# Queries, keys and u of an encoder layer: tokens stationary, 512 weight columns moving, then a turn on TensorE

## The chip, the cores and the metric

The kernel runs on one core of a Trainium2 chip. The metric is the device time of one execution in microseconds, the median of several runs. A core has five engines that are used here: TensorE (PE; its weight loads are listed apart as PEld), VectorE (DVE), ScalarE (ACT), GpSimd (POOL) and SyncE (SP), which issues the transfers from HBM. Each engine works through its own instructions in a fixed order and waits on semaphores for the others. TensorE writes to PSUM, which has eight banks of 128 partitions by 512 float32 here; four of them form two accumulators of 1024 columns, four are single banks.

## What is computed

One layer of an encoder on 256 tokens of width 2048, in float32. Cut to what matters here:

```python
h = rmsnorm(x, norm1_g)
z = h @ w_in                      # (256, 2048) @ (2048, 9216)
u_a, v_a, q, k, v_b, gate_logits = jnp.split(z, splits, axis=-1)   # u, v, q, k, v_b: 1024 columns each
a = spatial_gating(u_a, v_a, ...)                 # u = gelu(u); v = layernorm(gelu(v)); u * (W_s v + b_s)
o = diff_attention(q, k, v_b, lam, slopes)        # 8 heads, two score maps each, softmax(p0) - lam * softmax(p1)
gates = sigmoid(gate_logits + b_gate)
x = x + (gates[0] * (a @ w_proj_a) + gates[1] * (rmsnorm(o) @ w_proj_b)) @ w_out
x = x + hier_moe(rmsnorm(x), ...)                 # 16 experts, top 2 of the best group; final norm
```

## The kernel before

All weights are streamed from HBM once, in blocks of 128 x 2048 float32 (1 MB), in the order of use, into 27 "slots" of that size in SBUF, which activations share. A slot is given back when its content has been used, and the stream takes the slot that has been idle longest; a transfer waits until the last reader of its slot is done. SP issues all transfers in one order.

Products are made from two levels: every weight block is split by ScalarE and VectorE into a high part (`L85`, a cast) and a low part (`L86`, what is left), into a ring of three buffers, half a block at a time. The normalized tokens are kept in the same way (`hh`, `hl`). A product is then three matmuls: high by high, and each high by the other's low.

`z = h @ w_in` is made in groups of 512 columns. A group reads four blocks, 16 steps of 128 rows of the weights (k-steps). There are two forms:

- `cols_group` (lines 255 to 269, for queries, keys and u): 128 weight columns are stationary and the 256 tokens move (`L264`). A step is 12 matmuls of 256 columns, a group 192. The result has columns of z on the partitions and tokens along the free axis, as attention and the gating want it. VectorE multiplies it by the norm's factor `rb` (one per token, copied to all partitions): `L316`, `L325`, `L401`.
- `toks_block` (lines 271 to 281, for v_b, v, the gates, and later projections): 128 tokens are stationary and 512 weight columns move (`L280`). A step is 6 matmuls of 512 columns, a group 96. The result has tokens on the partitions; the norm's factor is a scalar per partition (`rcol`, made from `rb` by two tiny matmuls `L251`).

The groups come in the order q0, k0, v_b0, q1, k1, v_b1, v0, v1, u0, u1, then eight groups of gates. Queries and keys are written in two levels (`q2`, `k2`, `kl`; `L319`, `L320`, `L328` to `L330`). Between the groups the code starts the eight attention heads (`head`, lines 342 to 377): eight score matmuls (`L349`, `L350`), a softmax on VectorE and ScalarE in two buffers s0 and s1, four transposes (`L368`, wT), a split into wh and wl, six matmuls (`L375`, oT). s0, s1, wh, wl and other temporaries come from the pool `wk`, which has two buffers and hands them out in the order of the code. The spatial gating follows (`L420`, "mixed"), on u.

A scheduler orders each engine's instructions when the program is built: the code's order sets which buffers follow which, and an instruction comes up as soon as the scheduler thinks its inputs ready. After head 7 the slots of queries and keys are given back; the gates' biases (`L518`, bias_rows, four transfers to one of these slots) and the sixth and following blocks of the gates' weights go there.

Of the kernel before, what the change touches and what calls it, by code (L numbers as in the profile page):

```python
# [9 lines left out]
F32 = mybir.dt.float32  # L10
# [3 lines left out]
AF = mybir.ActivationFunctionType  # L14
OP = mybir.AluOpType
# [3 lines left out]
S = 256  # L19
NK = D // 128  # L20
# [76 lines left out]
def encoder(ctx, tc, A, out, stop=None):  # L97
    nc = tc.nc
    V, SC, PE, GP = nc.vector, nc.scalar, nc.tensor, nc.gpsimd
# [62 lines left out]
    stream = Stream(nc, slots, blocks)  # L162
# [40 lines left out]
    ident = consts.tile([128, 128], F32, name="ident")  # L203
# [15 lines left out]
    hh = [t[0].rearrange("p (k t) -> p k t", k=8) for t in hTh]  # L219
    hl = [t[0].rearrange("p (k t) -> p k t", k=8) for t in hTl]  # L220
    rb = dead_tile((S,))
    rcol = consts.tile([128, 2], F32, name="rcol")

    def x_in(c):

        half = xT[c // 4][0][:, c % 4 * 512:c % 4 * 512 + 512]
        nc.sync.dma_start(half, A["xT"].rearrange("p k t -> p (k t)")[:, c * 512:(c + 1) * 512])
        for k in range(2 * c, 2 * c + 2):
            i, kk = divmod(k, 8)
            SC.activation(hh[i][:, kk], xv[i][:, kk], AF.Copy, scale=g1[:, k:k + 1])  # L230
            V.scalar_tensor_tensor(hl[i][:, kk], xv[i][:, kk], g1[:, k:k + 1], hh[i][:, kk].bitcast(F32),
                                   op0=OP.mult, op1=OP.subtract)
# [19 lines left out]
                      skip_group_check=True)  # L252
        V.tensor_copy(rcol, rp[:, :2])

    def cols_group(xh, xl, nk, n_blocks, first_of_all=False):

        ps = acc()
        for b in range(n_blocks):
            for k, wh, wl in stream.parts((lambda k: x_in(2 * b + k // 2)) if first_of_all else None, first_of_all and b == 0):
                kk = b * 4 + k  # L260
                a, al = xh[kk // 8][:, kk % 8], xl[kk // 8][:, kk % 8]
                for w, v, first in ((wh, a, True), (wh, al, False), (wl, a, False)):
                    for j in range(4):
                        PE.matmul(ps[:, j * S:(j + 1) * S], w[:, j * 128:(j + 1) * 128], v,  # L264
                                  start=kk == 0 and first and j % 2 == 0,
                                  stop=kk == nk - 1 and w is wl and j % 2 == 1, skip_group_check=True)
        if first_of_all:
            x_norm()
        return ps.rearrange("p (j t) -> p j t", j=4)

    def toks_block(ps, xh, xl, b, nb):

        for k, wh, wl in stream.parts():
            kk = b * 4 + k
            a, al = xh[kk // 8][:, kk % 8], xl[kk // 8][:, kk % 8]
            steps = [(v, w, t) for v, w in ((a, wh), (a, wl), (al, wh)) for t in range(2)]
            if kk == nb * 4 - 1:
                steps.sort(key=lambda s: s[2])
            for v, w, t in steps:
                PE.matmul(ps[:, t * 512:(t + 1) * 512], v[:, t * 128:(t + 1) * 128], w,  # L280
                          start=kk == 0 and v is a and w is wh, stop=kk == nb * 4 - 1 and v is al)

    rb4 = rb[:, None, :].to_broadcast([128, 4, S])

    def z_cols(first_of_all=False):
        return cols_group(hh, hl, NK, 4, first_of_all)

    def toks_group(xh, xl, nb):

        ps = acc()  # L290
        for b in range(nb):
            toks_block(ps, xh, xl, b, nb)
        return ps.rearrange("p (t n) -> p t n", t=2)

    def z_toks():
        return toks_group(hh, hl, 4)

    view = lambda s, k: s[0].rearrange("p (k n) -> p k n", k=k)

# [3 lines left out]
    half = slice(0, 64), slice(64, 128)  # L303
    heads = slots.take()
    oT = view(heads, 8)
# [5 lines left out]
    vh, vl = view(vhs, 2), view(vls, 2)  # L311

    def evac_q(i):
        c = slice(4 * i, 4 * i + 4)
        q = oT[:, c]
        V.tensor_tensor(q, z_cols(i == 0), rb4, op=OP.mult)  # L316
        for m in range(2):
            a, b = half[m], half[1 - m]
            SC.copy(q2[m][a, c], q[a])  # L319
            V.tensor_tensor(q2[m][b, c], q[a], q2[m][a, c].bitcast(F32), op=OP.subtract)  # L320

    def evac_k(i):
        c = slice(4 * i, 4 * i + 4)
        k = oT[:, c]
        V.tensor_tensor(k, z_cols(), rb4, op=OP.mult)  # L325
        for m in range(2):
            a, b = half[m], half[1 - m]
            SC.copy(k2[m][a, c], k[a])  # L328
            SC.copy(k2[m][b, c], k[a])
            V.tensor_tensor(kl[m][a, c], k[a], k2[m][a, c].bitcast(F32), op=OP.subtract)  # L330

    def evac_vb(i):
        ps = z_toks()
# [627 lines left out]
```

## Time and profile before

| | |
|---|---|
| median of 3 runs | 1084.84 us (1083.54 to 1085.14) |
| the profiled execution | 1083.54 us |
| its span, first to last instruction | 1081.6 us |
| TensorE with work | 1048.3 us, 97% |
| weight loads | 700.1 us, 65% |
| VectorE, ScalarE | 510.0 us (47%), 395.9 us (37%) |
| read from HBM | 320.25 MB, 298 GB/s over the span |
| first half (norm, z, attention, gating, projections) | to about 622 us |
| experts | from about 630 us |

The rows that are shown below name an instruction by its line, engine, operation and operands (out<-in), with a count (x) and times in microseconds, or nanoseconds where it says so. "Busy" of TensorE counts a matmul to a modelled end, and matmuls overlap; how fast they follow each other is read from their starts. In square brackets stands how long the engine was idle before, and whom it waited for.

### The profile page before, as it was taken

Reading aid. Unit: us, or ns where it says so; the run is one execution under the profiler, and the core shown is the slowest. Engines: PE = TensorE matmul, PEld = TensorE weight load, DVE = VectorE, ACT = ScalarE, POOL = GpSimd, SP = SyncE. Lnnn points to the kernel's source line nnn. Section 1 sums busy time; section 2 is a strip of 40 time slices with the busy share of each in tenths; the row PEclk is TensorE's granted clock in tenths of the full one; section 3 lists DMA queues with packets and bytes.
Section 4 is the critical chain, followed back from the end, with each engine's and each line's share of the span. In section 5 each row is a group of like instructions: output and inputs, shape, how many; then the busy total and the mean of one; then the engine's idle time right before and its main releaser. Section 6 shows DMA issues by size and latency. Waiting matters only on the chain. (4 is left out here: it accounts for less than half of the span.)

```text
span 1081.6 us, 13529 instructions
## 1 busy us (share of the span) xinstructions
PE 1048.3 (97%) x5436; PEld 700.1 (65%) x5436; DVE 510.0 (47%) x745; ACT 395.9 (37%) x554; POOL 9.1 (1%) x16
## 2 busy tenths in 40 slices
PE   7999999999999999999999999999999998999995
PEld 7989988998788888888887743444434432333331
DVE  8775676866778655566655541312313111122121
ACT  7564555555566444444443320211211101111112
POOL 1000000000000000000000000000000000000000
PEclk9999999999999999999999999999999999999997
DMA  9914455455875656556964769999999999999994
GB/s 338 420 61 171 156 197 190 158 209 181 272 265 191 228 192 231 191 203 248 364 254 160 299 269 422 421 421 421 422 421 421 420 421 421 421 422 421 420 421 188
DMA packets 48642, 323.29 MB, mean 299 GB/s; under 512 B 5664, under 2 KB 5824, under 8 KB 11072
## 3 DMA queue, kind: packets, MB, share of 16 engines
q1 hardware_dynamic: 48576, 322.39, 76.3%
q8 instruction: 44, 0.72, 0.3%
q14 instruction: 22, 0.18, 0.0%
HBM read 320.25 MB, written 2.11 MB: 298 GB/s over the span
## 5 line engine op out<-in xcount | busy, mean ns | idle before, releaser
L280 PE MATMUL acc<-slot,slot 128*128 128x512 f32 x1920 | 445.2, 391 | 1.1 <-ACT slot L85 0.6
L280 PEld LDWEIGHTS acc<-slot,slot 128*128 128x128 f32 x1920 | 358.2, 188 | 75.2 <-DVE slot L86 1.0
L86 DVE TENSOR_TENSOR slot<-slot,slot 128x1024 fp32r<-128x1024 f32 (+1 forms) x210 | 253.9, 1211 | 166.0 <-ACT slot L85 165.0
L85 ACT CAST slot<-slot 128x1024 fp32r<-128x1024 f32 (+1 forms) x210 | 218.5, 1042 | 254.1 <-PE acc L280 182.1
L763 PE MATMUL s<-slot,slot 128*64 128x512 f32 x1024 | 228.3, 596 | 3.7 <-DMA slot<-in_w_dram 3.7
L763 PEld LDWEIGHTS s<-slot,slot 128*64 128x64 f32 x1024 | 70.1, 137 | 138.3 <-issue 118.5
L264 PE MATMUL acc<-slot,slot 128*128 128x256 f32 x1152 | 143.5, 286 | 6.0 <-ACT slot L85 5.9
L264 PEld LDWEIGHTS acc<-slot,slot 128*128 128x128 f32 x1152 | 140.8, 193 | 7.0 <-ACT slot L85 6.1
L817 PE MATMUL ye<-slot,slot 128*64 128x512 f32 x512 | 122.6, 604 | 4.7 <-DMA slot<-in_w_dram 3.6
L693 DVE TENSOR_TENSOR slot<-slot,slot 128x256 fp32r<-128x256 f32 x64 | 26.3, 419 | 136.8 <-PE gather L696 122.0
L817 PEld LDWEIGHTS ye<-slot,slot 128*64 128x64 f32 x512 | 31.6, 136 | 79.7 <-issue 39.4
L692 ACT CAST slot<-slot 128x256 fp32r<-128x256 f32 x64 | 25.6, 407 | 153.6 <-PE gather L696 143.6
L827 DVE SCALAR_TENSOR_TENSOR yl<-ye,slot_c,yh 128x512 fp32r<-128x512 f32 x32 | 24.0, 750 | 115.8 <-ACT yh L826 115.8
L826 ACT ACTIVATE yh<-ye,slot_c 128x512 fp32r<-128x512 f32 x32 | 22.0, 688 | 129.1 <-PE y L792 129.1
L696 PEld LDWEIGHTS gather<-slot 128*128 128x128 f32 x256 | 32.9, 189 | 19.8 <-issue 19.5
L700 DVE SCALAR_TENSOR_TENSOR slot<-gather,g,slot 128x256 f32<-128x256 f32 x64 | 27.9, 477 | 27.5 <-PE gather L696 27.3
L696 PE MATMUL gather<-slot 128*128 128x256 f32 x256 | 39.5, 296 | 0.0
L728 DVE TENSOR_TENSOR g<-g,s 64x512 f32<-64x512 f32 x16 | 11.1, 691 | 32.5 <-ACT g L727 32.4
L792 PEld LDWEIGHTS y<-yh,slot 128*128 128x128 f32 x64 | 9.6, 188 | 25.6 <-issue 24.8
L727 ACT ACTIVATE g<-s 64x512 f32<-64x512 f32 x16 | 9.5, 591 | 42.7 <-PE s L763 38.9
L792 PE MATMUL y<-yh,slot 128*128 128x512 f32 x64 | 23.7, 452 | 0.3 <-ACT yh L826 0.3
L792 PE MATMUL y<-yl,slot 128*128 128x512 f32 x64 | 20.2, 397 | 0.1
(191 smaller groups left out, 482.1 us busy)
## 6 DMA issues: line engine op xcount, KB each, us to landing
slot<-in_w_dram SPq DMA_DIRECT2D x192, 1024.0 KB, 19.8
slot<-in_w_in_dram SPq DMA_DIRECT2D x68, 1024.0 KB, 4.9
slot<-in_w_out_dram SPq DMA_DIRECT2D x16, 1024.0 KB, 5.0
slot<-in_w_proj_a_dram SPq DMA_DIRECT2D x8, 1024.0 KB, 4.9
slot<-in_w_proj_b_dram SPq DMA_DIRECT2D x8, 1024.0 KB, 4.8
slot<-in_w_in_dram SPq DMA_DIRECT2D x6, 512.0 KB, 8.1
slot<-in_xT_dram SPq DMA_DIRECT2D x8, 256.0 KB, 7.7
slot<-bias_rows SPq DMA_DIRECT2D x8, 256.0 KB, 6.3
```

What stands on the lines that cost most here:

```text
L85: nc.scalar.copy(h, w)
L86: nc.vector.tensor_tensor(l, w, h.bitcast(F32), op=OP.subtract)
L264: PE.matmul(ps[:, j * S:(j + 1) * S], w[:, j * 128:(j + 1) * 128], v, start=kk == 0 and first and j % 2 == 0, stop=kk == nk - 1 and w is w ...
L280: PE.matmul(ps[:, t * 512:(t + 1) * 512], v[:, t * 128:(t + 1) * 128], w, start=kk == 0 and v is a and w is wh, stop=kk == nb * 4 - 1 and ...
L692: SC.copy(s[:, :, 0], x)
L693: V.tensor_tensor(s[:, :, 1], x, s[:, :, 0].bitcast(F32), op=OP.subtract)
L696: mm = PE.matmul(ps[:, k * S:(k + 1) * S], s[:, t, i], d[:, t], start=k == t == i == 0, stop=k == t == i == 1, skip_group_check=True)
L700: out = V.scalar_tensor_tensor(xg[:, k], ps[:, k * S:(k + 1) * S], g2[:, kk:kk + 1], r_row, op0=OP.mult, op1=OP.mult)
L763: mm = PE.matmul(ps[i * CAP:(i + 1) * CAP], xg[:, k, j * CAP:(j + 1) * CAP], w[:, i, k], start=b == k == 0, stop=b == 7 and k == 1)
L792: PE.matmul(ya[:, t], PT[:, p, t * 128:(t + 1) * 128], y, start=n < 3 and p == 0 and y is ys[0], stop=p == NE // 2 - 1 and y is ys[1])
L817: mm = PE.matmul(ps[j * CAP:(j + 1) * CAP], hid[:, b * 2 + k, j * CAP:(j + 1) * CAP], w[:, j, k], start=b == 0 and k == 0, stop=b == 1 and ...
L827: V.scalar_tensor_tensor(yl, ps, sc, yh.bitcast(F32), op0=OP.mult, op1=OP.subtract)
```

## The change

Queries, keys and u are now made in the second form, with tokens stationary and 512 weight columns moving. `cols_group` is gone, and `toks_block` also serves the first group, whose weights and tokens arrive in pieces. Of each accumulator ScalarE reads both halves of 128 tokens into a pair of buffers z from the pool `wk`, times `rcol`, through a plain copy or, for u, the Gelu. TensorE transposes z in eight blocks of 128 x 128 into two single banks (zT). From these the two levels of queries and keys are made, and u is copied. The second copy of the keys' high part is made by VectorE from the first and no longer by ScalarE.

```diff
-    def cols_group(xh, xl, nk, n_blocks, first_of_all=False):
-
-        ps = acc()
-        for b in range(n_blocks):
-            for k, wh, wl in stream.parts((lambda k: x_in(2 * b + k // 2)) if first_of_all else None, first_of_all and b == 0):
-                kk = b * 4 + k
-                a, al = xh[kk // 8][:, kk % 8], xl[kk // 8][:, kk % 8]
-                for w, v, first in ((wh, a, True), (wh, al, False), (wl, a, False)):
-                    for j in range(4):
-                        PE.matmul(ps[:, j * S:(j + 1) * S], w[:, j * 128:(j + 1) * 128], v,
...
-    def toks_block(ps, xh, xl, b, nb):
-
-        for k, wh, wl in stream.parts():
+    def toks_block(ps, xh, xl, b, nb, first_of_all=False):
+
+        for k, wh, wl in stream.parts((lambda k: x_in(2 * b + k // 2)) if first_of_all else None, first_of_all and b == 0):
             kk = b * 4 + k
             a, al = xh[kk // 8][:, kk % 8], xl[kk // 8][:, kk % 8]
             steps = [(v, w, t) for v, w in ((a, wh), (a, wl), (al, wh)) for t in range(2)]
...
+    def z_toks(first_of_all=False):
+        ps = toks_group(hh, hl, 4, first_of_all)
+        if first_of_all:
+            x_norm()
+        return ps
+
+    def z_turned(func, first_of_all=False):
+
+        ps, z = z_toks(first_of_all), [wk(name="z") for _ in range(2)]
+        for t in range(2):
+            SC.activation(z[t], ps[:, t], func, scale=rcol[:, t:t + 1])
+        for h in range(2):
+            tp = bank("zT").rearrange("p (j t) -> p j t", j=2)
+            for t in range(2):
+                for j in range(2):
+                    c = (2 * h + j) * 128
+                    PE.transpose(tp[:, j, t * 128:(t + 1) * 128], z[t][:, c:c + 128], ident)
+            yield slice(2 * h, 2 * h + 2), tp
...
     def evac_q(i):
-        c = slice(4 * i, 4 * i + 4)
-        q = oT[:, c]
-        V.tensor_tensor(q, z_cols(i == 0), rb4, op=OP.mult)
-        for m in range(2):
-            a, b = half[m], half[1 - m]
-            SC.copy(q2[m][a, c], q[a])
-            V.tensor_tensor(q2[m][b, c], q[a], q2[m][a, c].bitcast(F32), op=OP.subtract)
+        for r, q in z_turned(AF.Copy, i == 0):
+            c = slice(4 * i + r.start, 4 * i + r.stop)
+            for m in range(2):
+                a, b = half[m], half[1 - m]
+                SC.copy(q2[m][a, c], q[a])
+                V.tensor_tensor(q2[m][b, c], q[a], q2[m][a, c].bitcast(F32), op=OP.subtract)
 
     def evac_k(i):
...
-            SC.copy(k2[m][a, c], k[a])
-            SC.copy(k2[m][b, c], k[a])
-            V.tensor_tensor(kl[m][a, c], k[a], k2[m][a, c].bitcast(F32), op=OP.subtract)
+        for r, k in z_turned(AF.Copy):
+            c = slice(4 * i + r.start, 4 * i + r.stop)
+            for m in range(2):
+                a, b = half[m], half[1 - m]
+                SC.copy(k2[m][a, c], k[a])
+                V.tensor_copy(k2[m][b, c], k2[m][a, c].bitcast(F32))
+                V.tensor_tensor(kl[m][a, c], k[a], k2[m][a, c].bitcast(F32), op=OP.subtract)
...
     def gelu_u(i):
-        V.tensor_tensor(uT[:, 4 * i:4 * i + 4], z_cols(), rb4, op=OP.mult)
-        SC.activation(uT[:, 4 * i:4 * i + 4], uT[:, 4 * i:4 * i + 4], AF.Gelu_apprx_tanh)
+        for r, u in z_turned(AF.Gelu_apprx_tanh):
+            V.tensor_copy(uT[:, 4 * i + r.start:4 * i + r.stop], u)
```

The lines of the changed kernel stand seven lower: its matmuls of all groups are `L264`, the reads into z `L284`, the transposes `L290`, the heads' transposes `L361`, the bias rows `L511`.

TensorE after the first key group of the changed kernel. z is the pair of buffers, acc the accumulator of the next group (v_b0), slot_72 to slot_74 the ring of split weights, slot_80 to slot_83 the tokens. The rows are those after 23 and after 46 matmuls of that group:

```order
L264 MATMUL acc<-slot_2_73,slot_7_80 128x512 x4
L264 MATMUL acc<-slot_2_73,slot_9_82 128x512 x2
...
L264 MATMUL acc<-slot_3_74,slot_9_82 128x512
L290 MATMUL zT<-ident,z 128x128 x4
L264 MATMUL acc<-slot_3_74,slot_9_82 128x512
...
L264 MATMUL acc<-slot_2_73,slot_7_80 128x512 x4
L290 MATMUL zT<-ident,z 128x128 x4
L264 MATMUL acc<-slot_2_73,slot_9_82 128x512 x2
```

The transposes of a group stand inside the next group, here in two parts; before the change the next group ran on without them.

TensorE around heads 6 and 7, before. s_2365 belongs to head 6, s_2412 to head 7; scores read the slots of queries and keys (slot_102 to slot_108), acc is a gate group:

```order
L368 MATMUL wT<-ident,s_2365 128x128 x4
...
L280 MATMUL acc<-slot_1_72,slot_8_81 128x512
L375 MATMUL oT<-wh,slot_18_111 128x256
...
L349 MATMUL scores<-slot_15_106,slot_13_104 128x256
L350 MATMUL scores<-slot_17_108,slot_13_104 128x256
L280 MATMUL acc<-slot_1_72,slot_8_81 128x512 x3
...
L280 MATMUL acc<-slot_3_74,slot_9_82 128x512 x2
L368 MATMUL wT<-ident,s_2412 128x128 x4
```

The same place after. s_1889 belongs to head 6, s_1936 to head 7:

```order
L264 MATMUL acc<-slot_3_74,slot_9_82 128x512 x2
L361 MATMUL wT<-ident,s_1889 128x128 x4
L368 MATMUL oT<-wh,slot_18_111 128x256
...
L343 MATMUL scores<-slot_17_108,slot_13_104 128x256
L368 MATMUL oT<-wl,slot_18_111 128x256
...
L361 MATMUL wT<-ident,s_1936 128x128 x4
...
L413 MATMUL mixed<-slot_49_1191,slot_34_632 128x128 x2
L264 MATMUL acc<-slot_1_72,slot_7_80 128x512 x2
```

Before, 60 + 25 gate matmuls stand between the end of u1 and head 7's scores, and 35 between these scores and head 7's transposes. After, 62 + 58 stand ahead of head 6's transposes, and none between head 7's scores and its transposes.

SP around the gates' biases, before and then after. bias_rows go to slot_70; slot_76, 77 and 78 are the sixth, seventh and eighth block of the gates:

```order
L71 DMA slot_78_2681<-in_w_in_dram 128x2048
L518 DMA slot_70_2451<-bias_rows 128x512 x4
L71 DMA slot_76_2621<-in_w_in_dram 128x2048
L71 DMA slot_77_2651<-in_w_in_dram 128x2048
L71 DMA slot_83_2874<-in_w_in_dram 128x2048
```

```order
L71 DMA slot_83_2398<-in_w_in_dram 128x2048
L71 DMA slot_78_2205<-in_w_in_dram 128x2048
L511 DMA slot_70_1975<-bias_rows 128x512 x4
L71 DMA slot_76_2145<-in_w_in_dram 128x2048
L71 DMA slot_77_2175<-in_w_in_dram 128x2048
```

One later block (slot_83) has moved ahead of the four slots that wait for head 7's scores.

## Rows read from the trace of the kernel before

**Rows 1.** The page: the busy line, and GB/s in 40 slices of 27 us
```profile
PE 1048.3 (97%) x5436; PEld 700.1 (65%) x5436; DVE 510.0 (47%) x745; ACT 395.9 (37%) x554; POOL 9.1 (1%) x16
...
GB/s 338 420 61 171 156 197 190 158 209 181 272 265 191 228 192 231 191 203 248 364 254 160 299 269 422 421 421 421 422 421 421 420 421 421 421 422 421 420 421 188
```

**Rows 2.** Windows: length, busy by engine, granted clock, DMA share, GB/s
```profile
300.00:350.00 50.00, 50.00 (x223) 41.30 (x222) 41.33 (x39) 34.12 (x39) 0.00 (x0) 1.00 0.67 221
...
626.00:628.00 2.00, 0.85 (x9) 0.73 (x8) 1.62 (x10) 0.00 (x0) 0.00 (x0) 1.00 0.00 0
```

**Rows 3.** Timeline of TensorE (start, length, instruction), key group and gates; one window
```profile
78.47 23.20 PE L264 MATMUL acc<-slot,slot 128*128 128x256 f32 x192
101.50 0.38 PE L368 MATMUL wT<-ident,s 128*128 128x128 f32 x2
...
249.13 13.79 PE L280 MATMUL acc<-slot,slot 128*128 128x512 f32 x60
262.76 0.60 PE L368 MATMUL wT<-ident,s 128*128 128x128 f32 x4
263.12 1.17 PE L280 MATMUL acc<-slot,slot 128*128 128x512 f32 x4
...
78.47:101.50 23.03, 23.03 (x193) 23.03 (x192) 11.19 (x10) 9.82 (x11) 0.00 (x0) 1.00 0.51 183
```

**Rows 4.** The first group: weight loads in the timeline, and one window
```profile
14.44 16.50 PEld L264 LDWEIGHTS acc<-slot,slot 128*128 128x128 f32 x137 [0.24 <-DVE slot L86]
30.86 0.30 PEld L243 LDWEIGHTS ssq<-slot,ones 128*128 128x128 f32 x2
...
6.00:9.00 3.00, 3.00 (x15) 3.00 (x16) 2.08 (x4) 2.36 (x5) 0.00 (x0) 1.00 1.02 327
```

**Rows 5.** Timeline at the projections' transposes; their line (ns min/median/max)
```profile
465.12 0.81 PE L545 MATMUL mT<-ident,slot 128*128 128x128 f32 x6
465.69 21.80 PE L280 MATMUL acc<-slot,slot 128*128 128x512 f32 x95
...
L545 PE MATMUL mT<-ident,slot x32: 270/272/273, 464.7 to 533.7; 128*128 128x128 f32 x32
```

**Rows 6.** Groups of instructions, 80 to 650 us: busy, mean ns, idle before
```profile
L130 DVE TENSOR_TENSOR slot<-mT,slot 128x512 fp32r<-128x512 f32 x8 | 5.2, 686 | 4.5 <-ACT slot L129 4.5
L397 ACT ACTIVATE slot<-acc,rcol 128x512 f32<-128x512 f32 x4 | 2.5, 686 | 2.2 <-PE acc L280 2.2
L330 DVE TENSOR_TENSOR slot<-slot,slot 64x1024 fp32r<-64x1024 f32 x2 | 2.4, 1214 | 0.0
L325 DVE TENSOR_TENSOR slot<-acc,slot 128x1024 f32<-128x1024 f32 x1 | 1.2, 1225 | 1.1 <-PE acc L264 1.1
```

**Rows 7.** Timeline of TensorE after head 7's scores
```profile
270.46 0.28 PE L350 MATMUL scores<-slot,slot 128*128 128x256 f32 x1
270.58 8.12 PE L280 MATMUL acc<-slot,slot 128*128 128x512 f32 x35
278.86 0.74 PE L368 MATMUL wT<-ident,s 128*128 128x128 f32 x4 [0.15 <-DVE s L366]
280.43 0.50 PE L375 MATMUL oT<-wh,slot 128*128 128x256 f32 x2 [0.83 <-ACT wh L129]
...
284.64 0.73 PE L280 MATMUL acc<-slot,slot 128*128 128x512 f32 x2 [0.55 <-ACT slot L85]
```

**Rows 8.** SP and ScalarE in the same stretch; block 76's issue and landing
```profile
270.80 2.24 SPq L518 DMA_DIRECT2D slot<-bias_rows  x4
...
283.54 1.99 ACT L85 CAST slot<-slot 128x1024 fp32r<-128x1024 f32 x2 [3.16 <-DMA slot<-in_w_in_dram]
...
L71 SPq DMA_DIRECT2D slot<-in_w_in_dram x1: 463/463/463, 273.1 to 273.1; - x1
...
DMA to landing us min/median/max: 10.4/10.4/10.4
```

**Rows 9.** The end: the last matmuls, and a window after them
```profile
1068.24 0.73 PE L792 MATMUL y<-yl,slot 128*128 128x512 f32 x2
...
1070.50:1071.00 0.50, 0.00 (x0) 0.00 (x0) 0.15 (x1) 0.50 (x2) 0.47 (x2) 0.50 0.00 0
```

More of the change, by code (lines that the diff above doesn't have):

```diff
@@ L253, in x_norm @@
         V.tensor_copy(rcol, rp[:, :2])
-    def cols_group(xh, xl, nk, n_blocks, first_of_all=False):
-        ps = acc()
-        for b in range(n_blocks):
-            for k, wh, wl in stream.parts((lambda k: x_in(2 * b + k // 2)) if first_of_all else None, first_of_all and b == 0):
-                kk = b * 4 + k
-                a, al = xh[kk // 8][:, kk % 8], xl[kk // 8][:, kk % 8]
-                for w, v, first in ((wh, a, True), (wh, al, False), (wl, a, False)):
-                    for j in range(4):
-                        PE.matmul(ps[:, j * S:(j + 1) * S], w[:, j * 128:(j + 1) * 128], v,
[L265 to L269, printed above, removed]
-    def toks_block(ps, xh, xl, b, nb):
-        for k, wh, wl in stream.parts():
+    def toks_block(ps, xh, xl, b, nb, first_of_all=False):
+        for k, wh, wl in stream.parts((lambda k: x_in(2 * b + k // 2)) if first_of_all else None, first_of_all and b == 0):
             kk = b * 4 + k
@@ L281, in toks_block, with toks_group @@
                           start=kk == 0 and v is a and w is wh, stop=kk == nb * 4 - 1 and v is al)
[L283 to L288, printed above, removed]
+    def toks_group(xh, xl, nb, first_of_all=False):
         ps = acc()
         for b in range(nb):
-            toks_block(ps, xh, xl, b, nb)
+            toks_block(ps, xh, xl, b, nb, first_of_all)
         return ps.rearrange("p (t n) -> p t n", t=2)
-    def z_toks():
-        return toks_group(hh, hl, 4)
+    def z_toks(first_of_all=False):
[14 more added lines that the diff above has]
+            yield slice(2 * h, 2 * h + 2), tp
     view = lambda s, k: s[0].rearrange("p (k n) -> p k n", k=k)
@@ L313, in evac_q @@
     def evac_q(i):
-        c = slice(4 * i, 4 * i + 4)
-        q = oT[:, c]
-        V.tensor_tensor(q, z_cols(i == 0), rb4, op=OP.mult)
-        for m in range(2):
-            a, b = half[m], half[1 - m]
-            SC.copy(q2[m][a, c], q[a])
-            V.tensor_tensor(q2[m][b, c], q[a], q2[m][a, c].bitcast(F32), op=OP.subtract)
-    def evac_k(i):
[L323 to L327, printed above, removed]
-            SC.copy(k2[m][a, c], k[a])
-            SC.copy(k2[m][b, c], k[a])
-            V.tensor_tensor(kl[m][a, c], k[a], k2[m][a, c].bitcast(F32), op=OP.subtract)
+        for r, q in z_turned(AF.Copy, i == 0):
[4 more added lines that the diff above has]
+                V.tensor_tensor(q2[m][b, c], q[a], q2[m][a, c].bitcast(F32), op=OP.subtract)
+    def evac_k(i):
+        for r, k in z_turned(AF.Copy):
[5 more added lines that the diff above has]
+                V.tensor_tensor(kl[m][a, c], k[a], k2[m][a, c].bitcast(F32), op=OP.subtract)
     def evac_vb(i):
```

## The prediction

> **What bounds the kernel now.** I read the busy line of the page and its slices, then windows by stage, then the order of instructions on TensorE where a stage leans on another engine. TensorE has work in 97% of the span, the other compute engines in less than half of it [rows 1]. The bytes moved by slice split the program in two: from the fourth slice to about 650 us they move 156 to 364 GB/s, after that they stand at 420 to 422 without a dip [rows 1]. So the second half, the experts, waits for weights. The first half is TensorE's own: from 300 to 350 us it is busy for all 50.00 us [rows 2]. Between the two, from 626 to 628 us, DMA moves nothing [rows 2]: the slots are full, and no new block is fetched before TensorE gives one back. The experts' transfers therefore start again when TensorE has finished the first half: a microsecond won or lost before 620 us is won or lost in the total. The change lies wholly before 300 us.
>
> **The change part by part.** Six groups change form (two each for queries, keys and u). A key group's 192 matmuls of 256 columns take 101.50 - 78.47 = 23.03 us, 119.9 ns each [rows 3]. Sixty matmuls of 512 columns, in the same program on weights split in the same way, take 262.76 - 249.13 = 13.63 us, 227.2 ns each [rows 3]; a turned group has 96 of them, 21.81 us. A group so gains 1.22 us. The rows show why the gain is small but not nothing: over the key group weight loads fill 23.03 of 23.03 us [rows 3], in a stretch of 512-column matmuls alone 41.30 of 50.00 [rows 2]; halving the number of loads takes them off the limit. Five groups gain 6.1 us. The first group starts behind its data: its last wait ends at 14.44 us on VectorE's low part, for the fifth of 16 k-steps, with 4 of that step's 12 matmuls left [rows 4]. The new order of a step wants the low part second and not last, so 4 of 6 are left there: 4 x 0.227 + 11 x 1.363 = 15.9 us, end at 30.35, against 30.86 in the row [rows 4]: 0.5 us. Together **-6.6 us**.
>
> The turning adds eight transposes a group, 48 in all. Four of them hold up TensorE's stream for 263.12 - 262.76 = 0.36 us, 90 ns each [rows 3]; six for 465.69 - 465.12 = 0.57, 95 ns [rows 5]. 48 x 92 ns is **+4.4 us**. Less than half of a 256-column matmul, 60 ns, it can hardly be: 2.9 is the low end.
> One transpose lasts 272 ns from its issue to its modelled end [rows 5]. The Trainium skill, "TensorE: Matmul & The Clock Gate", Part 4, gives some 275 ns for one in a kernel's context and says that the transposes do not count as activity for the clock. The duration agrees; the spacing shows that most of it overlaps. Charged in full it would be 13.2 us, a rival below.
>
> The new evacuations (two 128x512 ScalarE reads of the accumulator, 0.69 us each, then casts and subtractions from PSUM in halves, up to 0.69 us each [rows 6]) take the place of one 128x1024 product of 1.23 us and of 64-partition operations on 1024 columns, 1.21 us each on VectorE [rows 6]. Per key group VectorE gets 4 copies and 4 subtractions, at most 8 x 0.69 = 5.5 us for 3.7; ScalarE keeps half of its casts and gets the two reads. Both are half idle, and the work hides behind the 21.8 us of the next group if nothing queues badly. What queues: the splits of the coming weights (L85, L86) stand behind these operations on the same queues, and TensorE waits for the splits three parts later. After the two key groups I find the split ready about when it is wanted, within a microsecond. Against that stand waits of TensorE in the stretch before that may go. I take **+0.7 us**, from -0.5 to +5. The cover on TensorE itself is there: the order puts 23 matmuls, 5.2 us, between a group's end and its transposes, and the two ScalarE reads need 1.4.
>
> **The heads move, and that decides.** z takes both buffers of the pool `wk`, which the heads use for s0, s1 and then wh, wl. A head so waits for the turning before it, and the turning for the head before that. In the program's order head 0 comes in the fifth group and not in the third, and head 6 only after the last turning, 62 matmuls into the gates. Five blocks of weights, 120 matmuls, are in slots by then; the sixth (slot number 76) goes into a slot that holds queries, and its transfer stands on SP behind the four bias rows, which wait for head 7's scores. Before, 85 of the 120 matmuls precede these scores and 35 follow them, and cover head 7's softmax. Now all 120 precede them.
>
> After the last score is issued at 270.46, the next matmul that has its data starts at 284.64: 14.18 us [rows 7]. The bias rows are issued from 270.80, block 76 at 273.1, it needs 10.4 us to land, and ScalarE casts it at 283.54 after 3.16 us of waiting [rows 8]. The change alters nothing in this stretch: same transfers, same order, apart from one block that now goes ahead of it. But the 35 matmuls that lay inside are gone: **+7.95 us** (35 x 227.2 ns) of TensorE idle. Head 6's transposes also lose their cover: from the transposes to the first oT, unhidden, 280.43 - 278.86 = 1.57 us [rows 7] against the 0.36 of issue, less the 4 x 0.12 us of oT that move into the idle stretch: **+0.7 us**.
>
> The long idle stretch brings the clock in. After the last matmul pair, issued from 1068.24, the granted clock is 0.50 from 1070.5 on [rows 9]: from 2.4 to 1.2 GHz, within some 2 us of idling. The new stretch idles for about 7.9 us before head 7's transposes, so the clock falls in it. What the return costs I bound by the program's start, where TensorE comes out of idling: from 6 to 9 us 15 matmuls of 256 columns are seen [rows 4], where 25 fit at 119.9 ns; 10 fewer are 1.2 us, some of it waiting. I take **+1.0 us**, between 0 and 2.5 (twice the start's loss).
> The Trainium skill, same page, Part 1, says that half rate is the default and that activity releases it; the rows at the end agree on the fall. Without that rule the term would be 0 and the forecast 1092.0.
>
> **The sum**: -6.6 + 4.4 + 0.7 + 7.95 + 0.7 + 1.0 = +8.2 us. On the profiled execution's 1083.54 us (span 1081.6 and 1.9 around it) that is 1091.7. The median of the runs shown, 1084.84, lies 1.3 above the profiled one; the changed kernel will be given by a median, so I take 1084.84 + 8.2 = 1093.0. With all low ends (2.9 for the turning, no clock, -0.5 for queues) it is +4.5, 1089.3; with high ones (+5 for queues, 2.5 for the clock) +14, 1099.
>
> **Rivals.**
> Faster: the gap behind head 7 isn't longer. Then the three terms of the gap fall away, and -6.6 + 4.4 + 0.7 or a little less gives 1082.5 to 1083.3. It decides if block 76 lands within about 4 us of the scores (what wT, oT and the mixing products cover), where 12.8 are read now [rows 7, 8]. For it speaks that one block less competes; against it, that the block is issued behind the bias rows and these behind the scores, in both programs.
> About the same: the transfers of the gap, 3 MB, run at the 420 GB/s of full load and take 7.5 us for 12.8. Then 5.3 us come back: 1087.7, and with low ends within the margin. The bias rows are read in small pieces in both programs, which speaks against it.
> Slower by more: the turned groups themselves make TensorE wait, a microsecond or so at each of six turnings, as splits queue behind evacuations: 1098. For it, VectorE's queue after the key groups; against, 23 matmuls of cover.
> The change doesn't do what it says: 512 columns bring nothing in these groups, since what limits them is the supply of splits. Then 6.6 us are missing: 1099.6. Sixty matmuls at 227 ns between the same splits speak against it.
> The transposes cost their full duration, 48 x 272 ns = 13.1 us for 4.4: 1101.7. Rows 3 and 5 speak against it.
>
> **How the numbers follow.** The forecast 66%; faster 5%; about the same 7%; waits at the turnings 13%; no gain by 512 columns 5%; full transposes 4%. From 1088.5 to 1099.7 holds the forecast, the waits and nearly all of the case without a gain. About 0.2%, 2.2 us, is what a measurement of this kernel can tell from no change: slower than 1087.0 is 0.90 (all cases but the first two, and a part of the second), within 0.05, faster 0.05.
>
> **What would show it.** Right: matmuls of the turned groups at 227 ns; under 0.1 us of TensorE per transpose; all 120 gate matmuls before head 7's scores, then some 8 us in which TensorE does nothing, ended by a DMA, with a granted clock at half; from there to the end the same times as before, shifted. Wrong: the next gate matmul within 8 us of the scores; TensorE idle by ScalarE or VectorE for more than a microsecond at each turning; a first half that is later by less than its idle time has grown; or experts that end at 1081 although the first half ends later.

## The result

| | before | changed |
|---|---|---|
| median of six runs | 1084.8 us (1083.54 to 1085.14) | 1093.42 us (1093.13 to 1094.58) |
| the profiled execution, its span | 1083.54, 1081.6 us | 1093.47, 1091.6 us |
| TensorE with work | 1048.3 us | 1049.9 us |
| head 7's last score, first matmul on the next block | 270.46, 284.64 | 279.45, 294.81 |

The changed kernel is 8.6 us slower by the medians, a ratio of 1.0082 (95% interval 1.0071 to 1.0092); 1093.0 was forecast. The two profiled executions lie 9.9 us apart, because the one of before was the fastest of its runs.

The changed kernel's table of TensorE's waits (who waited for whom: us in total, times, longest) names the place.

```profile
PE wT L361 <- DVE s L359: 7.6, 1, 7.6
PE acc L264 <- ACT slot L85: 6.0, 1, 6.0
...
PE oT L368 <- ACT wh L129: 1.4, 2, 0.7
PE acc L264 <- DVE slot L86: 1.4, 3, 0.6
```

The 6.0 us are the start, 5.9 before. The 7.6 us are new: one single wait, head 7's transposes for head 7's softmax. The timeline of TensorE there answers [rows 7] (line numbers are 7 lower than before).

```profile
263.78 13.34 PE L264 MATMUL acc<-slot,slot 128*128 128x512 f32 x58
276.96 0.60 PE L361 MATMUL wT<-ident,s 128*128 128x128 f32 x4
278.28 0.50 PE L368 MATMUL oT<-wh,slot 128*128 128x256 f32 x2 [0.72 <-ACT wh L129]
...
279.45 0.28 PE L343 MATMUL scores<-slot,slot 128*128 128x256 f32 x1
...
287.78 1.09 PE L361 MATMUL wT<-ident,s 128*128 128x128 f32 x4 [7.57 <-DVE s L359]
289.59 0.79 PE L368 MATMUL oT<-wh,slot 128*128 128x256 f32 x2 [0.72 <-ACT wh L129]
...
294.81 0.71 PE L264 MATMUL acc<-slot,slot 128*128 128x512 f32 x2
```

The last 58 matmuls that have their data stand ahead of the scores, and none behind them. The bias rows and the next block go out as in [rows 8], only later:

```profile
279.79 2.16 SPq L511 DMA_DIRECT2D slot<-bias_rows  x4
281.99 13.88 SPq L71 DMA_DIRECT2D slot<-in_w_in_dram  x3
...
292.08 1.99 ACT L85 CAST slot<-slot 128x1024 fp32r<-128x1024 f32 x2 [2.54 <-DMA slot<-in_w_in_dram]
```

Windows of this stretch (length, busy by engine, granted clock, DMA share, GB/s) show the clock at half from about 284 to 294 us. The last one stands where [rows 2] had 626 to 628: the hole in the transfers before the experts has moved by 10 us and is as deep as it was. So the loss passes through to the end.

```profile
282.00:284.00 2.00, 0.00 (x0) 0.00 (x0) 1.14 (x4) 0.87 (x3) 0.00 (x0) 1.00 0.94 386
284.00:286.00 2.00, 0.00 (x0) 0.00 (x0) 1.03 (x2) 1.20 (x6) 0.00 (x0) 0.55 0.44 174
...
293.00:294.00 1.00, 1.00 (x6) 1.00 (x6) 0.85 (x1) 1.00 (x2) 0.00 (x0) 0.50 0.35 147
...
636.00:638.00 2.00, 0.90 (x5) 0.88 (x6) 1.61 (x10) 0.00 (x0) 0.00 (x0) 1.00 0.00 0
```

### The profile page after: what moved, and what is told of

Read it like the earlier page. It is cut to its first block, busy times and chain, and to the rows that moved or that the text cites. A ratio compares the mean times of both kernels' runs of the same rounds, so it can differ in the third digit from the quotient of the medians.

```text
span 1091.6 us, 12491 instructions
## 1 busy us (share of the span) xinstructions
PE 1049.9 (96%) x4908; PEld 678.3 (62%) x4908; DVE 511.7 (47%) x759; ACT 398.0 (36%) x568; POOL 9.1 (1%) x16
## 5 line engine op out<-in xcount | busy, mean ns | idle before, releaser
L264 PE MATMUL acc<-slot,slot 128*128 128x512 f32 x2496 | 582.3, 392 | 7.4 <-ACT slot L85 6.0
L264 PEld LDWEIGHTS acc<-slot,slot 128*128 128x128 f32 x2496 | 467.0, 188 | 105.2 <-ACT slot L85 6.0
L351 ACT ACTIVATE s<-s,mx 128x256 f32<-128x256 f32 x32 | 16.0, 500 | 5.4 <-DVE mx L349 5.1
L640 DVE TENSOR_SCALAR slot<-iota,place 128x64 fp32r<-128x64 f32 x32 | 5.8, 249 | 19.6 <-PE gather L689 19.6
```

## The experiments

The theory: the loss is the gap behind head 7's scores, and its size is the number of gate matmuls that are left to cover it; what the new form wins and costs in the groups is small beside it. The rival: the turnings cost the time, each its share. Every kernel is compared with runs of the kernel before that were made beside it (1084.07 to 1085.49 us).

| run | us | against before | 95% of the ratio | gate matmuls behind head 7's scores |
|---|---|---|---|---|
| changed kernel | 1093.42 | +8.6 | 1.0071 to 1.0092 | 0 |
| e10, before, heads later | 1094.10 | +10.0 | 1.0069 to 1.0100 | 0 |
| e3, only u turned | 1094.86 | +10.8 | 1.0078 to 1.0108 | 0 |
| e2, all but u turned | 1082.60 | -1.5 | 0.9980 to 0.9998 | 35 |
| e9, changed, heads earlier | 1084.38 | -1.1 | 0.9981 to 0.9999 | 58 |
| e9b, before, heads earlier | 1083.01 | -1.8 | 0.9973 to 0.9991 | 120 |
| e11, e2 with heads earlier | 1080.85 | -3.9 | 0.9951 to 0.9979 | 120 |
| e1, z out of the pool `wk` | 1092.84 | +7.4 | 1.0051 to 1.0082 | 2 |
| e1b, transposes into the accumulator | 1117.60 | +32.1 | 1.0275 to 1.0307 | 0 |
| e1c, both | 1098.29 | +12.8 | 1.0102 to 1.0133 | 28 |
| e5, gap filled with idle matmuls | 1092.63 | +7.8 | 1.0064 to 1.0091 | 0 |
| e6, each transpose twice | 1099.03 | +14.2 | 1.0113 to 1.0144 | 0 |
| e7a, bias rows ahead | 1092.25 | +7.4 | 1.0056 to 1.0087 | 0, a block fewer before them |

**The order alone makes the loss (e10).** Nothing is turned; only the heads are called later in the kernel before:

```diff
     evac_q(1)
-    head(0)
     evac_k(1)
-    head(1)
+    head(0)
     evac_vb(1)
-    head(2)
+    head(1)
...
     gelu_u(1)
+    head(5)
     head(6)
     head(7)
```

> The kernel before, nothing turned, with its heads called about one group later in the code, so that no gate matmul follows head 7's scores. Theory (the gap, and the order alone makes it): 35 x 0.227 = 7.95 us of cover lost, 0.7 for head 6's transposes, 0.8 to 1.0 for the clock: 1084.8 + 9.5 = 1094.3 (1093 to 1095.5). Rival (the stretch behind the scores shrinks when the stream is not running beside it): under 1090.

1094.10 us, 10.0 over the kernel before. TensorE's timeline is that of the changed kernel, with the same wait for the softmax:

```profile
279.57 0.28 PE L350 MATMUL scores<-slot,slot 128*128 128x256 f32 x1
...
287.87 1.09 PE L368 MATMUL wT<-ident,s 128*128 128x128 f32 x4 [7.53 <-DVE s L366]
...
290.27 3.62 PE L420 MATMUL mixed<-slot,slot 128*128 128x128 f32 x16
...
295.19 0.70 PE L280 MATMUL acc<-slot,slot 128*128 128x512 f32 x2
```

So a kernel with no transposes of z at all loses as much when its heads come late.

**Which turnings do it (e2, e3).** Either u or queries and keys are put back into the form of before.

```diff
# e2: all but u turned
-        for r, u in z_turned(AF.Gelu_apprx_tanh):
-            V.tensor_copy(uT[:, 4 * i + r.start:4 * i + r.stop], u)
+        V.tensor_tensor(uT[:, 4 * i:4 * i + 4], z_cols(), rb4, op=OP.mult)
+        SC.activation(uT[:, 4 * i:4 * i + 4], uT[:, 4 * i:4 * i + 4], AF.Gelu_apprx_tanh)
# e3: only u turned
-        for r, q in z_turned(AF.Copy, i == 0):
...
+        V.tensor_tensor(q, z_cols(i == 0), rb4, op=OP.mult)
```

> Queries and keys turned as in the changed kernel, u made as before with 128 columns stationary. Of the heads, 0 to 3 still wait for turnings, but behind v the chain has caught up: in the program's order 35 gate matmuls follow head 7's scores, as many as in the kernel before. Theory (the gap): the loss is gone although four of the six groups are turned: the kernel before's time and what the form nets in four groups, -0.5 - 3 x 1.22 + 32 x 0.092 + 0.5 = -0.7 by the sum on record, about 0 by e9 against e9b: 1084 to 1085.5 beside 1084.8. Rival (each turning costs its share of the loss): four sixths of 8.6, 1090.5.

> Only u is turned, queries and keys are made as before. The heads run as in the kernel before up to head 5; head 6 and 7 wait for the turnings of u, and no gate matmul follows head 7's scores. Theory (the gap): the whole loss is here, with two turned groups: 1084.8 + 7.95 + 0.7 + 0.8 (the clock, by the filled gap) = 1094, less up to 0.8 by the form: 1092.5 to 1094.5. Rival (each turning costs its share): two sixths of 8.6, 1087.7.

1082.60 and 1094.86 us; the first lies below its expected range, the second 0.4 above its own. TensorE's timelines, first two places of e2, then the long wait of e3:

```profile
248.96 13.79 PE L280 MATMUL acc<-slot,slot 128*128 128x512 f32 x60
...
284.31 0.73 PE L280 MATMUL acc<-slot,slot 128*128 128x512 f32 x2 [0.28 <-ACT slot L85]
```
```profile
289.09 1.09 PE L384 MATMUL wT<-ident,s 128*128 128x128 f32 x4 [7.47 <-DVE s L382]
```

Four turned groups lose nothing, two lose everything: it depends on which heads wait for them. Queries and keys are turned early, and the chain of heads catches up behind v; the turnings of u stand directly ahead of heads 6 and 7. That a turning costs its share is refuted on both sides. How much e2 wins is less sure: its trace is only 0.2 us ahead of the kernel before at the first gate matmul (249.13 in [rows 3]) and 0.3 at the next block (284.64 in [rows 7]). The profiled execution, 1084.96 us, is one of the slower of its eleven (1082.26 to 1085.40), and from the third gate group to the experts' first matmul it takes 330.1 us where the kernel before takes 327.5. Where the 1.5 us of the medians lie is not shown.

**The gap covered again (e9, e9b).** The heads are called one group earlier, in the changed kernel and, as a control, in the kernel before.

```diff
+    head(0)
     evac_q(1)
-    head(0)
+    head(1)
     evac_k(1)
-    head(1)
+    head(2)
...
     gelu_u(1)
-    head(6)
     head(7)
```

> The changed kernel with every head called one group earlier in the code (head 0 behind v_b0 instead of behind q1, head 7 behind u1); pools, turnings and all else as they are. 58 gate matmuls then follow head 7's scores, 13.2 us, and the bias rows and the next block are issued so much earlier against TensorE's work. Theory (the gap): of the 15.36 us between the last score and the first matmul on the next block some 3.0 us are head 7's own work at full clock, the other 12.3 are covered: 1093.4 - 12.3 = 1081.1 (1080.5 to 1083). Rival (the loss lies in the turnings): 1093. Second rival: the freed slots let the transfers start earlier but they are slower against other traffic, and half of the gap stays: 1087.

> The kernel before, with the same move of the heads one group earlier and nothing else; so it differs from e9 by the form of the six groups alone, with the gap covered in both. The kernel before idles 0.15 + 0.83 + 0.55 + 0.53 = 2.06 us between head 7's scores and the stream's return, e9 0.43 + 0.53 = 0.96 us, so the move is worth about 1.1 us here. Theory A (the form nets nothing: what 512 columns win the transposes and the first group's start eat up): as e9, 1.1 us below the kernel before, 1084.4 beside 1085.5. Theory B (the sum on record: the form nets -6.6 + 4.4 + 0.7 = -1.5 us): e9 is 1.5 us below this kernel, which then stands 0.4 above the kernel before at 1085.9, and the move of the heads is worth nothing in it. Theory C (the turnings cost more than the form wins): this kernel is below e9 by over 1 us, 1083 or less.

e9 takes 1084.38 us, 9.0 less than the changed kernel, or 9.7 if each is set against the runs of the kernel before beside it. 12.3 were forecast, and it lies above the expected 1080.5 to 1083; its profiled execution is 10.6 us shorter. The place is as expected: 58 matmuls lie behind the scores, the next block's split comes 0.43 us late.

```profile
266.13 13.34 PE L264 MATMUL acc<-slot,slot 128*128 128x512 f32 x58
279.31 0.60 PE L361 MATMUL wT<-ident,s 128*128 128x128 f32 x4
280.34 0.73 PE L264 MATMUL acc<-slot,slot 128*128 128x512 f32 x2 [0.43 <-ACT slot L85]
281.60 5.52 PE L264 MATMUL acc<-slot,slot 128*128 128x512 f32 x23 [0.53 <-DVE slot L86]
```

The expectation took all of the changed kernel's idle time there for winnable; these two waits stay, 0.96 us. Two more, of 0.6 and 0.5 us at the groups of u (below), are 0.2 us longer than the changed kernel's two; the other 0.5 of the 1.7 us that are missing in the profiled execution are not located. e9b takes 1083.01 us: 1.8 below the kernel before, and its trace shows no wait of TensorE between the start and 300 us; the 2.06 us that the kernel before idles in the gap are gone. Theory A had it 1.1 below, theory B 0.4 above, theory C over 1 us under e9; by differences it is 0.7 us under e9, and the two intervals overlap. That lies between A and C. e9's waits (2.08 us with those at the groups of u) are more than the 0.7, so the form might be ahead without them; no run took them away alone.

**What holds the heads (e1, e1b, e1c).** z gets idle space in the slots of the heads and of u (e1; u is then copied only after all eight transposes, since it lands in the same slot), or the transposes write into the accumulator that z was read from (e1b), or both (e1c).

```diff
# e1, e1c
-        ps, z = z_toks(first_of_all), [wk(name="z") for _ in range(2)]
+        ps, z = z_toks(first_of_all), z_space()
# e1b, e1c
-            tp = bank("zT").rearrange("p (j t) -> p j t", j=2)
+            tp = ps[:, h].rearrange("p (j t) -> p j t", j=2)
```

> The turned z no longer comes from the pool wk but from space that is idle (the slot of the heads for q0 and k0, the slot of u for the rest); the transposes still go to two of the four single banks. In the program's order head 0's scores stay behind the turning of q1, and only 2 gate matmuls follow head 7's scores (0 in the changed kernel, 35 in the kernel before). Theory: the time goes by the matmuls that are left to cover the gap behind head 7, so 2 x 0.227 = 0.5 us less than the changed kernel's 1093.4: 1092.9 (1092 to 1094). Rival A, by the words of the prediction alone: the pool wk is what holds the heads up, and with z out of it the time returns to 1083 to 1086. Rival B: the loss lies in the turnings themselves (transposes, evacuations, their queues) and not in the gap: 1093.

> The other half: z comes from the pool wk as in the changed kernel, but the transposes write into the accumulator that z was just read from, and not into the single banks. In the program's order no gate matmul follows head 7's scores. Theory (the gap): as the changed kernel, 1093.4 (1092.5 to 1094.5). Rival: the single banks alone hold the heads up: 1083 to 1086. The accumulator is held about 2 us longer; if that made TensorE wait at the turnings it would show as over 1095.

> Both halves together: z in space of its own, transposes into its own accumulator. Now head 0's scores stand in the third group again, and 28 gate matmuls follow head 7's scores. The turnings do all the same work. Theory (the gap): 28 x 0.227 = 6.4 us of the idle stretch are covered, and with an idle stretch of about 1 us before head 7's transposes most of the clock's 1 us goes too: 1093.4 - 6.4 - 1.0 = 1086.0 (1085 to 1087.5). Rival (the loss lies in the turnings): 1093, as the changed kernel.

e1 stays where it was. The pool `wk` alone isn't what holds the heads: the single banks are handed out in the order of the code too, and zT takes two of the four. e1c, which differs from e1 by the transposes' place alone, has head 0's scores in the third group again and 28 matmuls behind head 7's: with `wk` free, it is the banks that hold the heads. e1b shows nothing on the heads, since it brings waits of its own; two of the waits in its timeline that the changed kernel doesn't have:

```profile
59.98 13.91 PE L264 MATMUL acc<-slot,slot 128*128 128x512 f32 x50 [4.15 <-DVE slot L314]
...
168.16 9.42 PE L264 MATMUL acc<-slot,slot 128*128 128x512 f32 x28 [4.83 <-DVE slot L330]
```

A later group needs the accumulator while VectorE still reads zT or v_b from it. And the 28 matmuls behind the last wait take 9.42 us, 336 ns each, where 227 are usual: windows of its trace show a granted clock of 0.50 behind each of these waits. The Trainium skill, "Perfetto Trace Analysis", section "Optimizing Tensor Performance", advises to rotate matmul groups through different PSUM banks so that the reading of one overlaps the next; this run shows what it costs when a second use keeps an accumulator longer.

e1c missed its 1086.0 by 12 us, and in its total it tells nothing of the theory. Its trace says why. At k0's turning TensorE meets transposes and scores whose data isn't there:

```profile
56.84 0.65 PE L290 MATMUL acc<-ident,slot 128*128 128x128 f32 x4 [0.92 <-ACT slot L284]
60.08 0.58 PE L351 MATMUL scores<-slot,slot 128*128 128x256 f32 x1 [2.59 <-DVE slot L331]
...
61.66 7.61 PE L264 MATMUL acc<-slot,slot 128*128 128x512 f32 x22
...
281.30 0.28 PE L352 MATMUL scores<-slot,slot 128*128 128x256 f32 x1
...
296.92 8.92 PE L264 MATMUL acc<-slot,slot 128*128 128x512 f32 x26 [4.14 <-ACT slot L85]
```

The 22 matmuls behind that wait take 2.4 us more than at full clock. In the gap the 28 matmuls do lie behind the scores and the wait for head 7's softmax is gone, but the next block comes no sooner, 15.62 us behind the last score (15.36 in the changed kernel), TensorE idles 4.14 us for it, and then 26 gate matmuls run mostly at half rate (8.76 us start to start for 5.9). So 28 matmuls of cover did not keep the gap from costing here: the clock fell in the wait of 4.14 us. In the kernel before, whose waits in the gap are at most 0.83 us [rows 7], it did not: the 48 gate matmuls behind them take 11.06 us start to start, 230 ns each.

**The clock in the gap (e5).** Thirty matmuls that nobody reads, behind head 7's last score.

```diff
+                last = PE.matmul(scores[m][:, t], q, kl[m][:, h], start=False, stop=t == 1, skip_group_check=True)
+        if h == 7:
+            fill = bank("fill")
+            with tc.issue_after(last.ins):
+                for _ in range(30):
+                    PE.matmul(fill, ones_r, hTh[0][0][:, :512], start=True, stop=True)
```

> The changed kernel with 30 matmuls of 512 columns that nobody reads, put behind head 7's last score on TensorE: 6.8 us of the 7.57 in which it waits for head 7's softmax. No useful work moves. Theory (the clock costs about 1 us, and it is paid by head 7's oT and the mixing products, which run at half rate): the granted clock stays at 1.00 up to head 7's transposes, the 16 mixing products take 1.95 us as in the kernel before and not 3.62, and the first matmul on the next block comes when its split is ready, at 293.2 instead of 294.8: 1093.4 - 1.2 = 1092.2 (1091.8 to 1092.8). Rival (the clock costs nothing, the block is late anyway): 1093.4. Second rival (the filler runs past the softmax and delays head 7): 1094.

1092.63 us: 0.8 less than the changed kernel, in the expected range. Timeline of TensorE:

```profile
279.89 0.28 PE L343 MATMUL scores<-slot,slot 128*128 128x256 f32 x1
...
280.49 7.16 PE L348 MATMUL fill<-slot,ones 128*128 128x512 f32 x30
288.17 0.74 PE L366 MATMUL wT<-ident,s 128*128 128x128 f32 x4 [0.53 <-DVE s L364]
...
290.06 1.95 PE L418 MATMUL mixed<-slot,slot 128*128 128x128 f32 x16
...
293.45 0.73 PE L264 MATMUL acc<-slot,slot 128*128 128x512 f32 x2
294.70 11.22 PE L264 MATMUL acc<-slot,slot 128*128 128x512 f32 x48 [0.52 <-DVE slot L86]
```

A window of it, where the changed kernel reads 0.50:

```profile
286.00:288.00 2.00, 1.65 (x8) 0.98 (x6) 1.97 (x8) 1.16 (x1) 0.00 (x0) 1.00 1.01 270
```

The mixing products take 1.95 us for 3.62, and the first gate matmul comes 13.56 us behind the last score for 15.36. Of these 1.8 us the wait for the low part, which the slow products had hidden, takes 0.5 back.

**The price of a transpose (e6).** Each transpose of z is issued twice (`for _ in range(2)` around it).

> The changed kernel with each of the 48 transposes of z issued twice, to the same place. By the spacing of 92 ns: 48 x 0.092 = 4.4 us more, 1097.8 (1097 to 1098.5). Rival, the full duration of 272 ns: 13.1 us more, 1106.5. Rival, half of a 256-column matmul (60 ns): 2.9 us more, 1096.3.

1099.03 us, 5.6 over the changed kernel, 117 ns for each of the 48 (its runs lie between 1097.36 and 1100.30, which is 30 ns either way) and half a microsecond above the expected range. Two neighbouring starts in the two timelines, first the changed kernel, then e6, give the spacing: 0.79 us for 8, and 1.67 for 16.

```profile
105.16 1.03 PE L290 MATMUL zT<-ident,z 128*128 128x128 f32 x8
105.95 0.37 PE L342 MATMUL scores<-slot,slot 128*128 128x256 f32 x1
```
```profile
107.01 1.91 PE L291 MATMUL zT<-ident,z 128*128 128x128 f32 x16
108.68 0.36 PE L343 MATMUL scores<-slot,slot 128*128 128x256 f32 x1
```

So it is some 100 to 110 ns, near the forecast's 92 and far from the 272 ns that one lasts.

**The other end of the gap (e7a).** The bias rows are read ahead, into the slot that the layer norm's factors leave.

```diff
-    slots.give(lns)
     head(4)
+    bgs = lns
...
+    bias_in(0)
...
-            bgs = slots.take()
...
+            if i:
+                bgs = slots.take()
+                bias_in(i)
```

> The changed kernel with the four bias rows read ahead, behind head 4 in the code, into the slot that the layer norm's factors leave; so after head 7's scores the next block's transfer is the first on SP's queue and has no bias rows beside it. Heads, turnings and the cover are as in the changed kernel. Theory (the gap's length is set by bias rows and block together): the block is issued 2.2 us earlier and lands in some 5 us (the fastest landing in that stretch, 4.8) instead of 10 to 12, its split is ready about 287, the first matmul on it comes 7 to 8 us earlier: 1086 (1084.5 to 1088). Rival (the block lands as late without the bias rows): only the 2.2 us on the queue are won, 1091.2.

1092.25 us, 1.2 less than the changed kernel where 7 were expected: the gap got shorter and little was won. The timeline of TensorE:

```profile
273.20 0.28 PE L343 MATMUL scores<-slot,slot 128*128 128x256 f32 x1
...
282.17 1.22 PE L264 MATMUL acc<-slot,slot 128*128 128x512 f32 x2 [8.21 <-ACT slot L85]
```

From the last score to the next block are 8.97 us for 15.36, 6.4 less, as the theory had it. But the slot that holds the bias rows had held a block of weights: its 24 matmuls, 5.45 us, no longer stand ahead of the scores. The expectation priced the transfer and forgot the slot.

**The two gains together (e11).** e2's form and e9's order of the heads.

> The two edits that stood below the kernel before, in one kernel: queries and keys turned and u made as before (e2: 1.5 us below), and the heads called one group earlier (on the kernel before: 1.8 us below). In the program's order head 7's oT stands 4 matmuls behind the gates' second group, and none of its products waits for the next block. Theory (they add, since the one wins in the groups and the other in the gap): 3.3 us below the kernel before, 1081.0 beside 1084.3. Rival (they win the same microseconds, or the first was scatter of the runs): 1.5 to 1.8 below, 1082.6.

1080.85 us, 3.9 below the kernel before (ratio 0.9965, 0.9951 to 0.9979): by the medians they add, and this is the fastest kernel of the study. What queries and keys win doesn't show in the traces here either: e11's second gate group starts at 275.27, that of e9b at 275.87, and its first matmul, at 6.11 for 6.66 us, was already 0.55 ahead. Where the others have the gap, its timeline reads without a wait; the eight mixing products stand behind head 7's oT, and the next block is there:

```profile
272.84 1.78 PE L280 MATMUL acc<-slot,slot 128*128 128x512 f32 x7
274.46 1.05 PE L434 MATMUL mixed<-slot,slot 128*128 128x128 f32 x8
275.27 6.16 PE L280 MATMUL acc<-slot,slot 128*128 128x512 f32 x26
```

## Why the prediction was right, point by point

**The gap (+7.95): right.** It was the term that decided, and the order of the program showed it. The last score moved by 8.99 us, which holds the 35 matmuls, and no matmul of the stream is left in the stretch behind it. e10, e3 and e9 show the cause from three sides. One of its signs came out otherwise: the long wait, 7.57 us, is ended by head 7's softmax on VectorE and not by a DMA; the block's transfer lands behind it, while TensorE works at half rate.

**Why the heads are late: half right.** The prediction named the pool `wk`. e1 frees it, and the heads stay late; the banks hand the same order on. Nor do all turnings count: those of u alone do it (e3), those of queries and keys alone don't (e2). That one pool is enough by itself is shown for the banks alone (e1): with z in `wk` and the banks free (e1b) the program's order also leaves no cover, but its time is drowned in other waits. The prediction's number didn't rest on which pool it is.

**Head 6's cover (+0.7): right, if a little large.** The wait for wh at 278.28 is 0.72 us. From the transposes to the first oT are 278.28 - 276.96 = 1.32 us; by the prediction's own reckoning, less 0.36 and 4 x 0.12, that makes 0.5.

**The clock (+1.0): right in size; its place was named nowhere.** It is paid by head 7's oT and the mixing products, which run at half rate until 294, and not by the gate matmuls. From 293.1, when ScalarE has cast the first half of the next block, to 294.81 TensorE is still busy with them. e5 gives the price, 0.8 us by the medians (the runs of the two kernels overlap, 1092.35 to 1093.62 and 1093.13 to 1094.58), 1.8 - 0.5 = 1.3 in place. The bound from the program's start is weak: the window in [rows 4] reads a granted clock of 1.00, so the row by itself doesn't show that the clock slowed the matmuls there. The Trainium skill, "TensorE: Matmul & The Clock Gate", Part 1, has half rate as the default that activity lifts; the windows agree, 1.00 while the filler runs, 0.50 without it.

**The groups (-6.6 + 4.4 + 0.7 = -1.5): too good by some 2 us in the profiled pair.** Of the last score's 8.99 us 7.95 and 0.5 are accounted for; the remaining 0.5 are what the form cost up to there, where 1.5 were to be won. The matmuls themselves are as forecast: 169 of them from 66.72 to 105.16, 227.5 ns each, 227.2 in [rows 3]. The terms that were off:

- The first group: -0.5 forecast. In this pair its last wait ends at 14.99 instead of 14.44 in [rows 4], and the loads of the norm's product start at 31.24 instead of 30.86: +0.4. The pair is a poor witness, though. The next group's first matmul stands at 30.86 in the kernel before and at 31.57, 31.73 and 31.88 in the three others that make the first group in the old form (e9b, e3, e10); in the ten with the new form it stands at 30.79 to 31.40. By the starts of its matmuls TensorE reaches its full rate at 8.9 us in the kernel before, at 10.9 in the changed one and as late as 12 in others of either form. So the -0.5 is neither shown nor refuted.
- The transposes: 4.7 us by their spacing, for 4.4.
- The queues: 0.92 us of waits for low parts, in the place of 0.7, but elsewhere than at the turnings. They stand in u0's group and at the start of u1's. All nine kernels of the study that turn u have waits for splits there, one or two, of 0.6 to 2.0 us together; before, e2, e9b, e10 and e11, which make u as before, have none. In the changed kernel's timeline:

```profile
210.62 10.50 PE L264 MATMUL acc<-slot,slot 128*128 128x512 f32 x45 [0.58 <-DVE slot L86]
...
222.61 3.00 PE L264 MATMUL acc<-slot,slot 128*128 128x512 f32 x12 [0.34 <-DVE slot L86]
```

VectorE there works on the layer norm and head 4's softmax ahead of the splits (its timeline):

```profile
208.22 1.22 DVE L406 TENSOR_TENSOR slot<-slot,slot 128x1024 f32<-128x1024 f32 x1
209.35 1.21 DVE L86 TENSOR_TENSOR slot<-slot,slot 128x1024 fp32r<-128x1024 f32 x1
```

With these terms the groups come to 0.4 - 6.1 + 4.7 + 0.9 = -0.1 us, in the place of -1.5; the last score shows 0.5, and the 0.6 us between the two are not located.

The new order of a step wants the low part after two matmuls, 0.45 us; the old one after eight of 256 columns, 0.96 us. The waits of 0.3 to 0.6 us fit that difference; those of 0.7 to 0.9 us for the high part at u1's start, in e1, e1c, e3 and e6, it doesn't explain. No run changed the order of a step alone, so it is argued, not shown. e11 against e9 shows what u's turning costs altogether with the gap covered: 2.8 us, of which TensorE's four waits in e9 are 2.1. For queries and keys alone the form wins 1.5 us in e2 by the medians, where the same arithmetic gives -0.5 - 3 x 1.22 + 32 x 0.092 = -1.2 without queues; by e2's trace it is 0.2 to 0.3 up to the gap, so the size of the win is not shown.

**The base.** The sum gave 1091.7 for an execution like the profiled one, and 1.3 were added since that lay below its median. The profiled execution of the changed kernel took 1093.47, the median 1093.42. So the 8.2 us came close to the medians' 8.6 and are 1.7 short of the profiled pair's 9.9; by the places in the trace it is the second that the terms should have met. That 1093.0 lies so close to the median is in part luck: the 1.3 that was added for the base, and that the changed kernel's profiled execution doesn't ask for, stands in for most of what the groups didn't win.

**The rivals.** That the gap isn't longer, or that its transfers run at full rate, is refuted: the block took 10 us to land as before. Waits at the turnings came to nothing there. Full-length transposes are refuted by e6. That 512 columns bring nothing is refuted for the matmuls themselves by their 227.5 ns (two of 256 columns take 239.8 in [rows 3]); for the six groups together it is nearly what happened, since the transposes and the waits took back what the matmuls won.

## What to carry to other kernels

Where a chain of small work is spread over a stream of matmuls, a change that takes temporary buffers from the pools of that chain moves the chain, and what it then no longer covers can be many times what the change itself wins or costs: read in the new program's order how much work stands behind the last link before pricing instructions. A pool that is handed out in the order of the code suffices to hold it up, and freeing one of two did not help here (e1). The cure is cheap: eight heads called one place earlier in the code, worth 9 us. A transfer brought forward needs a place to land, and that place was somebody's buffer.

## What the runs showed of the hardware

- **The clock falls in short waits too.** In e1c TensorE waited 0.92 us and then 2.59 us, with four transposes and no more between them; windows of its trace show the granted clock fall from 2.4 towards 1.2 GHz while it waits, and the 22 matmuls behind the waits pay 2.4 us.

```profile
55.00:58.00 3.00, 1.57 (x11) 0.97 (x9) 0.40 (x2) 2.48 (x4) 0.00 (x0) 1.00 0.41 169
58.00:61.00 3.00, 0.69 (x2) 0.43 (x2) 2.91 (x5) 1.48 (x4) 0.00 (x0) 0.83 0.00 0
61.00:64.00 3.00, 3.00 (x9) 2.51 (x10) 2.49 (x5) 0.35 (x1) 0.00 (x0) 0.50 0.03 5
```

- **A transpose of 128 x 128 in a row of eight costs about 100 ns of TensorE's stream**, with another 48 of them 110 ns each, although each lasts 272.
